# Scores as full 128-row products, a first stage with feature-major x and 768 columns, values' products spaced by eight steps

## The chip, the core and the metric

The kernel runs on one core of a Trainium2 chip. The metric is the device time of one execution in microseconds; a time is the median of several runs. Five engines work side by side, each in the order of its own stream: TensorE (PE in the profile; its weight loads are shown apart as PEld), VectorE (DVE), ScalarE (ACT), GpSimd (POOL) and SyncE (SP), which here issues every DMA.

## What is computed

Two layers of a hybrid block on 1,024 tokens of width 2,048, in float32. Cut to what matters here:

```python
mod = silu(c) @ w_mod + b_mod                    # 2048 -> 6144
shift, scale, gate = split(mod, 3)
h = rms_norm(x, g_pre) * (1 + scale) + shift
proj = h @ w_in                                  # 2048 -> 5648, split into ten parts
# a: 16 query heads on 4 key heads of 64, rotary on 16 of 64, window of 128, sinks
scores = einsum('bnqgrd,bnkgd->bngrqk', qb, kb) * 64 ** -0.5     # key blocks n-1 and n
m = maximum(max(where(valid, scores, -inf)), sink);  p = exp(scores - m)
y_a = einsum('bngrqk,bnkgd->bnqgrd', p / (sum(p) + exp(sink - m)), vb)
# b: chunked spatial gating;  c: gated linear attention in chunks, with a normed output
y = concat(y_a, y_b, y_c) * silu(z)
x = x + gate * rms_norm(y @ w_out, g_post)       # then the second layer
```

## The kernel before

The tokens are cut into two halves of 512, and a **phase** is one layer on one half: four phases, each with an input part (`in_phase`, ten groups of products with `w_in`) and an output part (`out_phase`). A product of two float32 matrices is made as three TensorE products in the fp32r format: both operands are split into a high and a low part (ACT casts, DVE subtracts; L368/L369 for weights, L278/L279 for activations), and high x high, high x low and low x high are added up in one PSUM bank. `mm_f` (L382 to L384) gives features on partitions, `mm_t` (L390 to L392) gives tokens on partitions. Weights pass in slices of two 128-row tiles through `wraw` (two raw buffers) and `whl` (three split ones). One **step** is one call of `mm_f` or `mm_t`, three products; after each, `tick()` lets the side work go on.

**The side work** is written as generators that are stepped between products. Each `yield n` says after how many steps it goes on. The lane "att" holds the attention, "gla" the gated linear attention, "sg" the spatial gating, "mod" the later modulation, which DVE does. `drain` runs a lane to a given point at once. Within this, a scheduler may move an instruction ahead of others that aren't ready, and `urgent()` raises priorities; an engine then keeps the resulting order. All side products share two PSUM buffers, `mx`; the ten groups have six, `pj`. Temporary tiles `t2` have four buffers.

**Attention** (L477 to L556): for each of the eight head pairs of a phase, `bp` runs over two pairs of token blocks. The queries of a head are held as 64 rows of high and 64 rows of low parts (`qs`), so one 128-row product with the high keys `kh` (L493) gives high x high and low x high, and a 64-row product with the low keys `kl` (L497) adds high x low. `kl[j]` holds the keys of two heads, one in each half of the partitions. After the evictions (L503/L505 on ACT, L506 on DVE) come the softmax (L511 to L525), 14 steps later the transposes of the probabilities (L538) and their products with the masks (L540, on DVE), and `LAG["t"]` steps after each of the two the next piece: three steps between the two heads, five before the products with the values (L551). The attention of the second set of heads starts when that of the first is drained, at the end of the group q1. In the step that follows, the gated part loads its norm weights (L823) and multiplies by them on DVE (L825, L827) before its own transposes on TensorE (L563).

**The first stage** (L1011 to L1129) makes the modulation of layer 0 and the first group of phase 0 together. Silu of c is held as 32 equal columns (`scb`); 64 modulation tiles of 512 KB (`wm0`, nine buffers) give 128 products of 32 columns (L1112), 16 in each of eight chunks, on the four column quarters of one PSUM bank. After a chunk, ACT copies the sums, TensorE transposes them (L197), DVE adds them up and makes the columns `acol` and `bcol` for two 128-row tiles of activations (L199 to L205). x comes with tokens on partitions (`xg`): ACT squares it for the norm (L1059), POOL multiplies it by 1/rms (L283), TensorE transposes it (L1089), DVE applies the columns (L1091), and `split` makes the two parts. Each of the 16 activation tiles is then multiplied by five 128-column weight tiles: the four of the group kcq and the first half of the key weights of part c. The other half follows as a group of its own (`proj_f(P, slots)`, L785). The rotary tables of the half (`rope_tables`, 18 DVE operations with two sines on ACT) are emitted before the first products.

Of the kernel before, what the change touches and what calls it, by code (L numbers as in the profile page):

```python
# [21 lines left out]
P = 128  # L22
# [3 lines left out]
NH = 2  # L26
# [6 lines left out]
LAG = {"s": (3, 4), "e": 14, "t": (3, 5)}  # L33
# [3 lines left out]
WM0 = 9  # L37
# [3 lines left out]
def hybrid_kernel(ctx: ExitStack, tc: tile.TileContext, a, y_out):  # L41
# [82 lines left out]
    def rsqrt(out, src, n):  # L124

        i = sm.tile([P, n], I32, tag="rq_i", name="rq_i")
# [3 lines left out]
        for it in range(3):  # L130
            w = sm.tile([P, n], F32, tag="rq_w", name="rq_w")
            V.tensor_tensor(w, yv, yv, ALU.mult)
            V.scalar_tensor_tensor(w, w, -0.5, src, ALU.mult, ALU.mult)
            dst = out if it == 2 else sm.tile([P, n], F32, tag="rq_y", name="rq_y")
            V.scalar_tensor_tensor(dst, w, 1.5, yv, ALU.add, ALU.mult)
            yv = dst
# [156 lines left out]
    def h_filler_x(h, slots):  # L293
# [3 lines left out]
        def fetch():  # L297
            if len(xs) < NK:
                xt = io_tile()
                load(xt, a["x_f"][len(xs)])  # L300
# [152 lines left out]
    def split_keys(j, kr, first):  # L453
# [23 lines left out]
    def attention(l, h, g0, qt, vt, cst):  # L477
# [5 lines left out]
        for m in range(4):  # L483
# [3 lines left out]
            for bp in range(2):  # L487
                sps = [mxt().rearrange("p (b k) -> p b k", b=2) for _ in range(2)]
                for b in range(2):
                    n = 2 * bp + b  # L490
                    k0 = P if h == 0 and n == 0 else 0
                    for p in range(2):
                        PE.matmul(sps[p][:, b, k0:], lhsT=qs[:, p, n * P:(n + 1) * P],  # L493
                                  rhs=kh[2 * j + p][:, n * P + k0:n * P + 256], start=True, stop=False)
                    for p in range(2):
                        rows = slice(64 * p, 64 * p + 64)
                        PE.matmul(sps[p][:, b, k0:], lhsT=qs[rows, p, n * P:(n + 1) * P],  # L497
                                  rhs=kl[j][rows, n * P + k0:n * P + 256], start=False, stop=True)
# [256 lines left out]
    def in_phase(l, h, slots, pre=None):  # L755
# [29 lines left out]
        ps = ps[4:] + proj_f(P, slots) if pre else proj_f(256, slots)  # L785
        ck = evac(2, hold, ps)
# [213 lines left out]
    for l, h in phases:  # L1000
        G_ = [(a["w_in"][l, k], 512) for k in range(len(GROUPS))]
        seq = [G_[0], (a["w_ck"][l], 256), (a["w_vcg"][l], 272)] + G_[1:]
        if (l, h) == (0, 0):
            seq = [(a["w_ck"][l, :, :, P:], P)] + seq[2:]
# [7 lines left out]
    with tc.tile_pool(name="start", bufs=1) as st:  # L1012
        scb = st.tile([P, NK, 32], F32, name="scb")
        V.tensor_copy(scb, sc.unsqueeze(2).broadcast_to([P, NK, 32]))
        xg = [st.tile([P, 4, NT, P], F32, name=f"x0_{g}") for g in range(4)]
        ss0 = sm.tile([P, NT, 4], F32, tag="xss4", name="xss4")
        load(mb[0], a["b_mod_col"][0])
        load(gpc[0], a["g_pre"][0])
# [255 lines left out]
```

## Time and profile before

| | |
|---|---|
| time, median of 3 runs | 3167.28 us (3166.84 to 3167.59) |
| the profiled execution | 3170.71 us, its span 3169.0 us |
| HBM traffic | 429.37 MB read, 36.70 MB written |
| DMA engines, mean share | 47.8% |
| granted TensorE clock, mean | 0.99 |

A row of a timeline gives start, duration, engine, line, operation, output and input by the program's names, and the count of merged instructions; in brackets, the idle time before it and what ended that. The program issues a float32 product as two instructions, so that a pair of modulation products shows as x4. TensorE's durations overlap: the step from one start to the next is what a product costs. Idle time of an engine that isn't the bound costs nothing.

The 40 slices of the page show where DVE and the DMAs are loaded, and the clock in the first one:

```profile
DVE  3268777665676877745355676644346475653425
PEclk8999999999999999999999999999999999999999
DMA  9754446566676335544346322334446322333535
```

### The profile page before, as it was taken

To read this page: it belongs to the slowest core of one execution; us is meant where nothing else is said; L and a number is where in the kernel's file an instruction comes from. 1 tells how busy PE (TensorE), PEld (TensorE's weight loads), DVE (VectorE), ACT (ScalarE), POOL (GpSimd) and SP (SyncE) were. 2 spreads that over 40 slices of the span, in tenths; PEclk is the share of its full clock that TensorE was granted. 3 is DMA by queue.
4 is the path that set the end of the run, shared out by engine and by line. 5 is a ranking of instruction groups with operands and counts; after the bars stand their busy time and mean duration, and the time that the engine had idled before them with its cause. 6 is when DMAs were issued, how large, how long until landed. Compare 5 with 4: busy or idle time off the path is not lost.

```text
span 3169.0 us, 44364 instructions
## 1 busy us (share of the span) xinstructions
PE 3095.0 (98%) x17346; PEld 2459.1 (78%) x17346; DVE 1838.1 (58%) x2953; ACT 1207.0 (38%) x2399; POOL 41.3 (1%) x80
## 2 busy tenths in 40 slices
PE   6999999999999999999999999999999999999998
PEld 2477777888878777888888877788888877788886
DVE  3268777665676877745355676644346475653425
ACT  3144437332344444323234454432223544432323
POOL 2000000000000000000000000000000000000000
PEclk8999999999999999999999999999999999999999
DMA  9754446566676335544346322334446322333535
GB/s 330 231 162 135 134 129 194 184 194 205 199 232 193 118 115 164 181 142 149 120 120 188 94 75 89 111 112 135 121 125 203 97 83 84 103 120 111 165 103 167
DMA packets 224195, 468.99 MB, mean 148 GB/s; under 512 B 21584, under 2 KB 77296, under 8 KB 223984
## 3 DMA queue, kind: packets, MB, share of 16 engines
q1 hardware_dynamic: 223984, 466.15, 47.8%
q8 instruction: 136, 2.23, 0.3%
q14 instruction: 75, 0.61, 0.1%
HBM read 429.37 MB, written 36.70 MB: 147 GB/s over the span
## 4 chain that ended last, share of the span: by engine, by line
PE 82%; DVE 7%; DMA 7%; ACT 2%; issue 2%; SPq 0%; DVEq 0%; ACTq 0%
PE pj L382 13%; PE pj L383 12%; PE pj L384 12%; PE pj L390 12%; PE pj L392 11%; PE pj L391 11%; DMA wm<-in_w_mod_dram 4%; PE mx L551 2%; PE mx L497 2%; PE mx L493 1%; PE pj L1112 1%; DVE ma L225 1%; DVE whl L369 1%; DMA t<-in_gla_norm_g_dram 1%; PE mx L538 1%
## 5 line engine op out<-in xcount | busy, mean ns | idle before, releaser
L369 DVE TENSOR_TENSOR whl<-wraw,whl 128x1024 fp32r<-128x1024 f32 (+3 forms) x512 | 590.9, 1154 | 740.7 <-ACT whl L368 739.0
L368 ACT CAST whl<-wraw 128x1024 fp32r<-128x1024 f32 (+3 forms) x512 | 509.0, 994 | 1108.3 <-PE pj L392 508.5
L390 PE MATMUL pj<-whl,act 128*128 128x512 f32 (+1 forms) x2048 | 792.2, 387 | 1.4 <-ACT whl L368 1.0
L392 PE MATMUL pj<-whl,act 128*128 128x512 f32 (+1 forms) x2048 | 779.7, 381 | 0.0
L391 PE MATMUL pj<-whl,act 128*128 128x512 f32 (+1 forms) x2048 | 777.5, 380 | 1.1 <-DVE whl L369 1.1
L382 PE MATMUL pj<-act,whl 128*128 128x512 f32 x1904 | 753.8, 398 | 3.6 <-ACT whl L368 1.9
L384 PE MATMUL pj<-act,whl 128*128 128x512 f32 x1904 | 745.6, 392 | 1.3 <-DVE whl L369 1.2
L383 PE MATMUL pj<-act,whl 128*128 128x512 f32 x1904 | 744.8, 391 | 0.3 <-DVE act L279 0.3
L390 PEld LDWEIGHTS pj<-whl,act 128*128 128x128 f32 x2048 | 386.1, 189 | 79.6 <-issue 6.0
L392 PEld LDWEIGHTS pj<-whl,act 128*128 128x128 f32 x2048 | 386.1, 189 | 73.9 <-issue 0.7
L391 PEld LDWEIGHTS pj<-whl,act 128*128 128x128 f32 x2048 | 386.6, 189 | 69.7 <-DVE whl L369 1.7
L382 PEld LDWEIGHTS pj<-act,whl 128*128 128x128 f32 x1904 | 357.5, 188 | 103.9 <-issue 20.4
L384 PEld LDWEIGHTS pj<-act,whl 128*128 128x128 f32 x1904 | 358.0, 188 | 85.5 <-issue 7.3
L383 PEld LDWEIGHTS pj<-act,whl 128*128 128x128 f32 x1904 | 358.4, 188 | 77.4 <-issue 5.9
L225 DVE SCALAR_TENSOR_TENSOR ma<-wm,sc,ma 128x512 f32<-128x512 f32 x240 | 179.8, 749 | 107.6 <-DMA wm<-in_w_mod_dram 105.2
L522 ACT ACTIVATE M<-M,at_nm 128x128 f32<-128x128 f32 x256 | 99.4, 390 | 47.6 <-DVE at_nm L514 45.1
L506 DVE COPY_PREDICATED M<-pmask,mx 128x256 f32<-128x256 uint8 x128 | 51.6, 443 | 91.4 <-ACT M L505 79.0
L540 DVE TENSOR_TENSOR PT<-mx,amask 128x1024 f32<-128x1024 f32 x64 | 78.0, 1220 | 24.3 <-PE mx L538 24.2
L1112 PE MATMUL pj<-wm,scb 128*32 128x512 f32 x256 | 66.8, 666 | 24.5 <-DMA wm<-in_w_mod_dram 24.5
L505 ACT COPY M<-mx 128x256 f32<-128x256 f32 x96 | 32.0, 375 | 133.0 <-PE mx L497 132.9
L551 PE MATMUL mx<-PT,v 128*64 128x128 f32 x960 | 67.9, 287 | 12.1 <-DVE PT L540 12.1
L551 PEld LDWEIGHTS mx<-PT,v 128*64 128x64 f32 x960 | 57.2, 143 | 26.7 <-DVE PT L540 14.8
(229 smaller groups left out, 2391.4 us busy)
## 6 DMA issues: line engine op xcount, KB each, us to landing
wraw<-in_w_in_dram SPq DMA_DIRECT2D x312, 512.0 KB, 3.6
wraw<-in_w_out_dram SPq DMA_DIRECT2D x136, 512.0 KB, 3.6
wm<-in_w_mod_dram SPq DMA_DIRECT2D x256, 256.0 KB, 3.3
wm<-in_w_mod_dram SPq DMA_DIRECT2D x64, 512.0 KB, 6.2
y<-at SPq DMA_DIRECT2D x64, 256.0 KB, 2.6
q<-y SPq DMA_DIRECT2D x64, 256.0 KB, 3.3
q<-x SPq DMA_DIRECT2D x36, 256.0 KB, 2.8
wraw<-in_w_vcg_dram SPq DMA_DIRECT2D x32, 272.0 KB, 2.8
```

Source lines behind the costliest of these rows:

```text
L225: V.scalar_tensor_tensor(acc, ws[k], sc[:, k:k + 1], acc, ALU.mult, ALU.add)
L368: S.copy(hl[:, 0], raw)
L369: V.tensor_tensor(hl[:, 1], raw, hl[:, 0].bitcast(F32), ALU.subtract)
L382: PE.matmul(ps, lhsT=whi, rhs=slot[:, 0], start=(k == 0), stop=False)
L383: PE.matmul(ps, lhsT=whi, rhs=slot[:, 1], start=False, stop=False)
L384: PE.matmul(ps, lhsT=wlo, rhs=slot[:, 0], start=False, stop=(k == NK - 1))
L390: PE.matmul(ps, lhsT=slot[:, 0, c], rhs=whi, start=(k == 0), stop=False)
L391: PE.matmul(ps, lhsT=slot[:, 0, c], rhs=wlo, start=False, stop=False)
L392: PE.matmul(ps, lhsT=slot[:, 1, c], rhs=whi, start=False, stop=(k == NK - 1))
L522: S.activation(Mf[:, k], Mf[:, k], AF.Exp, bias=nm[:, k:k + 1], scale=0.125, accum_out=den[:, k:k + 1])
L551: PE.matmul(yp[64 * p:64 * p + 64, n * P:(n + 1) * P], lhsT=vv[:, g * 64:g * 64 + 64], rhs=pts[p][:, w, n], start=(w == 0), stop=(w == 1 o ...
L1112: PE.matmul(mps[r:r + 32, :], lhsT=scb[:, k], rhs=w[:, kk], start=(k < 4), stop=(k >= 12))
```

## The change

Three edits, which the diff shows with their core.

1. **Scores.** The low keys get a tile for each head, `kl[g]`, whose other 64 partitions are set to zero once. The product with the low keys is then 128 rows high as well, with the same `qs` as the one with the high keys, and stands right behind it.
2. **First stage.** x comes with features on partitions (`x_f`, now for both halves of the tokens), two tiles in one load, ahead of the modulation. The squares are added up by TensorE products with ones (L1057), and 1/rms is made on DVE for 512 columns at once. Scaling, columns and split are three operations per tile (`fill`). The modulation tiles have twelve buffers; a chunk's products are emitted in two blocks of eight with projection steps between them. Each activation tile meets six weight tiles (768 columns), so the group of its own for the c-keys' second half goes. The rotary tables are emitted after chunk 1.
3. **Spacing.** `LAG["t"]` goes from (3, 5) to (3, 8).

```diff
-LAG = {"s": (3, 4), "e": 14, "t": (3, 5)}
+LAG = {"s": (3, 4), "e": 14, "t": (3, 8)}
-WM0 = 9
+WM0 = 12
...
-        if not first:
-            V.tensor_copy(kl[j][:, 0:P], kl[j][:, H:H + P].bitcast(F32))
-        for p in range(2):
-            r = slice(64 * p, 64 * p + 64)
-            V.tensor_tensor(kl[j][r, P:], kr[r], kh[2 * j + p][r, P:].bitcast(F32), ALU.subtract)
+            if not first:
+                V.tensor_copy(kl[g][r, 0:P], kl[g][r, H:H + P].bitcast(F32))
+            V.tensor_tensor(kl[g][r, P:], kr[r], kh[g][r, P:].bitcast(F32), ALU.subtract)
...
                     for p in range(2):
-                        PE.matmul(sps[p][:, b, k0:], lhsT=qs[:, p, n * P:(n + 1) * P],
-                                  rhs=kh[2 * j + p][:, n * P + k0:n * P + 256], start=True, stop=False)
-                    for p in range(2):
-                        rows = slice(64 * p, 64 * p + 64)
-                        PE.matmul(sps[p][:, b, k0:], lhsT=qs[rows, p, n * P:(n + 1) * P],
-                                  rhs=kl[j][rows, n * P + k0:n * P + 256], start=False, stop=True)
+                        for part, keys in enumerate((kh, kl)):
+                            PE.matmul(sps[p][:, b, k0:], lhsT=qs[:, p, n * P:(n + 1) * P],
+                                      rhs=keys[2 * j + p][:, n * P + k0:n * P + 256], start=(part == 0), stop=(part == 1))
...
-        ps = ps[4:] + proj_f(P, slots) if pre else proj_f(256, slots)
-        ck = evac(2, hold, ps)
+        ck = evac(2, hold, ps[4:] if pre else proj_f(256, slots))
...
+        xq = [act_p.tile([P, 2, H], F32, tag="act", name="xq") for _ in range(8)]
+        for c in range(8):
+            load(xq[c], a["x_f"][0, 2 * c:2 * c + 2].rearrange("j p t -> p j t"))
...
+        def mod_load(c, qs=range(8)):
+            if c < 8:
+                for q in qs:
+                    w = st.tile([P, 2, 512], F32, name="wm0", bufs=WM0)
+                    load(w, a["w_mod"][0, c, :, 2 * q:2 * q + 2])
+                    ws.append(w)
+        mod_load(0)
         first_load(0)
-        for g in range(4):
-            for t in range(NT):
-                S.activation(junk_tile().rearrange("p (j c) -> p j c", j=4), xg[g][:, :, t], AF.Square,
-                             accum_out=ss0[:, t, g:g + 1])
-        finish_stats(0, 0, ss0)
-        psk = [pjt() for _ in range(5)]
-        mps = pjt()
+        mod_load(1, range(4))
+
+
+        sums = mxt()
+        for c in range(8):
+            sq = st.tile([P, 2, H], F32, name="sq", bufs=2)
+            S.activation(sq, xq[c], AF.Square)
+            s2 = st.tile([P, H], F32, name="s2", bufs=2)
+            V.tensor_tensor(s2, sq[:, 0], sq[:, 1], ALU.add)
+            PE.matmul(sums, lhsT=ones, rhs=s2, start=(c == 0), stop=(c == 7))
+        r0 = st.tile([P, H], F32, name="r0")
+        V.tensor_scalar(r0, sums, 1.0 / D, EPS, ALU.mult, ALU.add)
+        rsqrt(r0, r0, H, st)
+        psk = [pjt() for _ in range(6)]
...
-                    for m in range(5):
+                    for m in range(6):
                         mm_f(psk[m], hls[m // 4], k2, m % 4, slots[k], k)
...
-        def tail(c, acc):
-
-            mod_columns(0, c, acc, 4)
-            yield
-            for j in (2 * c, 2 * c + 1):
-                pt = mxt()
-                for t in range(NT):
-                    PE.transpose(pt[:, t * P:(t + 1) * P], xg[j // 4][:, j % 4, t], ident)
-                v = t2()
-                V.tensor_scalar(v, pt, acol[0][:, j:j + 1], bcol[0][:, j:j + 1], ALU.mult, ALU.add)
-                slots.append(split(v))
-                yield
...
+        def columns(c, mps):
             acc = st.tile([P, 512], F32, name="mod_acc", bufs=2)
+            S.copy(acc, mps)
+            mod_columns(0, c, acc, 4)
+
+        def fill(c):
+            for j in range(2):
+                k = 2 * c + j
+                xt, b = t2(), bcol[0][:, k:k + 1]
+                V.scalar_tensor_tensor(xt, xq[c][:, j], acol[0][:, k:k + 1], r0, ALU.mult, ALU.mult)
+                s = act_p.tile([P, 2, 512], F32R, tag="act", name="act")
+                S.activation(s[:, 0], xt, AF.Identity, bias=b)
+                V.scalar_tensor_tensor(s[:, 1], xt, b, s[:, 0].bitcast(F32), ALU.add, ALU.subtract)
+                slots.append(s)
...
+        for c in range(8):
+            mps = mxt()
+            mod_products(mps, 0)
+            if c:
+                go(5)
+            mod_load(c + 1, range(4, 8))
+            if c == 0:
+                first_load(1)
+            mod_products(mps, 1)
+            mod_load(c + 2, range(4))
             with urgent():
-                S.copy(acc, mps)
-            go(2)
-            rest = tail(c, acc)
-            if c in (0, 7):
-                for _ in rest:
+                columns(c, mps)
+                fill(c)
+            if c:
+                go(7)
+            if c == 1:
+                for _ in rope_tables(0):
                     pass
+        go(12)
         for _ in todo:
             pass
...
-    kl = [pools["kk"].tile([P, P + H], F32R, name=f"kl{j}") for j in range(2)]
+
+    kl = [pools["kk"].tile([P, P + H], F32R, name=f"kl{g}") for g in range(4)]
+    for g in range(4):
+        G.memset(kl[g][64 - 64 * (g % 2):P - 64 * (g % 2)].bitcast(F32), 0.0)
```

What this does to the order of the instructions is shown at three places. A row gives the line, the operation, output and input, the size of the operand that is streamed and, where a row stands for several alike, their number; the program issues each product of float32 as two instructions, which such a row counts once.

**Scores, on TensorE**, the end of the first head pair's scores in phase 0. `kh` and `kl` are the high and low keys, `pj` a projection's bank, `act` and `whl` split activations and weights; L390 to L392 are projection products. Before:

```order
L493 MATMUL mx<-kh_1195,qs 128x128
L493 MATMUL mx<-kh_1196,qs 128x128
L497 MATMUL mx<-kl_1199,qs 128x128 x2
L493 MATMUL mx<-kh_1195,qs 128x256
L493 MATMUL mx<-kh_1196,qs 128x256
L497 MATMUL mx<-kl_1199,qs 128x256 x2
L390 MATMUL pj<-whl,act 128x512
```

With the change, the second half of that pair:

```order
L492 MATMUL mx<-kh_1167,qs 128x256
L492 MATMUL mx<-kl_1171,qs 128x256
L492 MATMUL mx<-kh_1168,qs 128x256
L492 MATMUL mx<-kl_1172,qs 128x256
L492 MATMUL mx<-kh_1167,qs 128x256
L492 MATMUL mx<-kl_1171,qs 128x256
L390 MATMUL pj<-whl,act 128x512
```

Each head now has its own low keys, and products with high and low keys alternate; both are 128 rows high.

**First stage, on TensorE**, behind the modulation of chunk 2 (counted from 0). L197 transposes its sums, L1089 transposes tiles of x, L1112 and L1087 are modulation products, L382 to L384 the first group's projection products. Before:

```order
L197 MATMUL mx<-ident,mod_acc 128x128 x4
L382 MATMUL pj<-act,hl_b 128x512
L1112 MATMUL pj<-wm_444,scb 32x512 x2
L383 MATMUL pj<-act,hl_b 128x512
L384 MATMUL pj<-act,hl_b 128x512
L1089 MATMUL mx<-ident,x_1_170 128x128
L1112 MATMUL pj<-wm_448,scb 32x512 x2
L1089 MATMUL mx<-ident,x_1_170 128x128 x7
L1112 MATMUL pj<-wm_463,scb 32x512 x2
L382 MATMUL pj<-act,whl 128x512 x3
```

With the change:

```order
L197 MATMUL mx<-ident,mod_acc 128x128 x4
L1087 MATMUL mx<-wm_395,scb 32x512 x2
L1087 MATMUL mx<-wm_397,scb 32x512 x2
L1087 MATMUL mx<-wm_399,scb 32x512 x2
L1087 MATMUL mx<-wm_401,scb 32x512 x2
L1087 MATMUL mx<-wm_509,scb 32x512 x2
L1087 MATMUL mx<-wm_511,scb 32x512 x2
L1087 MATMUL mx<-wm_513,scb 32x512
L382 MATMUL pj<-act,whl 128x512 x4
```

Where the rest of the chunk before and eight transposes of x, with two modulation pairs among them, stood between the transposes of the sums and the chunk's first projection product, six and a half pairs of the next chunk's modulation now stand.

On DVE, L158 to L176 are the rotary tables and L205 makes `acol`, the last of a chunk's columns. Before, behind chunk 0's columns:

```order
L205 SCALAR_TENSOR_TENSOR acol_103<-mod_t,gpc_109 128x2
L158 CAST t_196<-t_196 128x512
L159 TENSOR_SCALAR t_196<-t_196,fcol 128x512
L163 TENSOR_SCALAR t_200<-t_196 128x512
L164 TENSOR_SCALAR t_200<-t_200 128x512
```

With the change, the end of the rows between chunk 2's columns and the scaling of its first tile (L1098), which its first projection product needs:

```order
L164 TENSOR_SCALAR t_463<-t_463 128x512
L170 SCALAR_TENSOR_TENSOR t_455<-t_451,t_455 128x512
L165 TENSOR_SCALAR t_463<-t_463 128x512
L173 TENSOR_SCALAR t_455<-t_455 128x512
L168 SCALAR_TENSOR_TENSOR t_467<-t_463,t_447 128x512
L174 TENSOR_SCALAR t_455<-t_455 128x512
L1098 SCALAR_TENSOR_TENSOR t_546<-xq,acol_103,r_256 128x512
```

The tables have moved from behind chunk 0's columns to behind chunk 2's: fourteen of their operations, eight of them ahead of these rows, stand between L205 and L1098.

**Second attention of phase 0.** On TensorE, `PT` are the masked transposed probabilities, `v` the values, and `ident,hold` marks the transposes of the gated part. Before, its values' products and those transposes:

```order
L551 MATMUL mx<-PT,v 64x128
L390 MATMUL pj<-whl,act 128x512
L391 MATMUL pj<-whl,act 128x512
L551 MATMUL mx<-PT,v 64x128 x13
L392 MATMUL pj<-whl,act 128x512
L563 MATMUL mx<-ident,hold 128x128
```

With the change:

```order
L558 MATMUL mx<-ident,hold 128x128 x2
L390 MATMUL pj<-whl,act 128x512
L391 MATMUL pj<-whl,act 128x512
L392 MATMUL pj<-whl,act 128x512
L546 MATMUL mx<-PT,v 64x128 x14
L558 MATMUL mx<-ident,hold 128x128 x4
```

On DVE, `t_3930` and `t_3801` are the loaded norm weights. Before, around the head pair's second mask product:

```order
L540 TENSOR_TENSOR PT<-mx,amask 128x1024
L825 SCALAR_TENSOR_TENSOR hold<-hold,t_3930 128x512
L540 TENSOR_TENSOR PT<-mx,amask 128x1024
L827 TENSOR_TENSOR hold<-hold 128x512
L825 SCALAR_TENSOR_TENSOR hold<-hold,t_3930 128x512
```

With the change:

```order
L535 TENSOR_TENSOR PT<-mx,amask 128x1024
L225 SCALAR_TENSOR_TENSOR ma<-wm,sc,ma 128x512
L819 SCALAR_TENSOR_TENSOR hold<-hold,t_3801 128x512 x2
L821 TENSOR_TENSOR hold<-hold 128x512
L369 TENSOR_TENSOR whl<-wraw,whl 128x1024
L821 TENSOR_TENSOR hold<-hold 128x512
L819 SCALAR_TENSOR_TENSOR hold<-hold,t_3801 128x512
L225 SCALAR_TENSOR_TENSOR ma<-wm,sc,ma 128x512
L821 TENSOR_TENSOR hold<-hold 128x512
L535 TENSOR_TENSOR PT<-mx,amask 128x1024
```

The values' products have moved behind eight of the transposes, the first of which stands 31 projection products behind the end of q1's group, and the second mask product behind three of the gated part's products with the weights. The first attention of the phase, for its part, is still drained at the end of q1: in phases 1 to 3 its last softmax is followed by that end after 40 projection products, where it was 54.

More of the change, by code (lines that the diff above doesn't have):

```diff
@@ L123, in hybrid_kernel, with rsqrt @@
     load(fcol, a["k_fcol"])
-    def rsqrt(out, src, n):
-        i = sm.tile([P, n], I32, tag="rq_i", name="rq_i")
+    def rsqrt(out, src, n, pool=sm):
+        i = pool.tile([P, n], I32, tag="rq_i", name="rq_i")
         V.tensor_scalar(i, src.bitcast(I32), 1, None, ALU.logical_shift_right)
@@ L130, in rsqrt @@
         for it in range(3):
-            w = sm.tile([P, n], F32, tag="rq_w", name="rq_w")
+            w = pool.tile([P, n], F32, tag="rq_w", name="rq_w")
             V.tensor_tensor(w, yv, yv, ALU.mult)
             V.scalar_tensor_tensor(w, w, -0.5, src, ALU.mult, ALU.mult)
-            dst = out if it == 2 else sm.tile([P, n], F32, tag="rq_y", name="rq_y")
+            dst = out if it == 2 else yv
             V.scalar_tensor_tensor(dst, w, 1.5, yv, ALU.add, ALU.mult)
@@ L299, in fetch @@
                 xt = io_tile()
-                load(xt, a["x_f"][len(xs)])
+                load(xt, a["x_f"][1, len(xs)])
                 xs.append(xt)
@@ L1012, in hybrid_kernel @@
     with tc.tile_pool(name="start", bufs=1) as st:
+        load(mb[0], a["b_mod_col"][0])
+        load(gpc[0], a["g_pre"][0])
+        xq = [act_p.tile([P, 2, H], F32, tag="act", name="xq") for _ in range(8)]
+        for c in range(8):
+            load(xq[c], a["x_f"][0, 2 * c:2 * c + 2].rearrange("j p t -> p j t"))
         scb = st.tile([P, NK, 32], F32, name="scb")
         V.tensor_copy(scb, sc.unsqueeze(2).broadcast_to([P, NK, 32]))
[L1015 to L1018, printed above, removed]
         ws = deque()
@@ L1024, in first_load @@
                 k = slice(c * KC, (c + 1) * KC)
-                pool, tag = (st, "raw_a") if c % 3 == 2 else (wraw_p, "wraw")
-                r = pool.tile([P, KC, 512], F32, tag=tag, name="raw_a")
+                r = wraw_p.tile([P, KC, 512], F32, tag="wraw", name="raw_a")
                 load(r, a["w_in"][0, 0, :, k])
                 raw_a.append(r)
-                r = st.tile([P, KC, P], F32, name="raw_b", bufs=3)
-                load(r, a["w_ck"][0, :, k, 0:P])
+                r = st.tile([P, KC, 256], F32, name="raw_b", bufs=2)
+                load(r, a["w_ck"][0, :, k])
                 raw_b.append(r)
@@ L1034, in first_split @@
             if c < 8:
-                for raw, hls, cols in ((raw_a, hl_a, 512), (raw_b, hl_b, P)):
+                for raw, hls, cols in ((raw_a, hl_a, 512), (raw_b, hl_b, 256)):
                     r = raw.popleft()
-                    if cols == P:
-                        hl = st.tile([P, 2, KC, P], F32R, name="hl_b", bufs=2)
+                    if cols == 256:
+                        hl = st.tile([P, 2, KC, cols], F32R, name="hl_b", bufs=2)
                     else:
-                        hl = whl_p.tile([P, 2, KC, 512], F32R, tag="whl", name="whl")
+                        hl = whl_p.tile([P, 2, KC, cols], F32R, tag="whl", name="whl")
                     S.copy(hl[:, 0], r)
```

45 lines of the change are left out of this document (11 added, 34 removed).

## The prediction

> **What bounds the kernel now.** I read the page first, then the list of TensorE's waits, then the timeline of TensorE at the three places that the change touches.
>
> ```profile
> span 3169.0 us, 44364 instructions
> PE 3095.0 (98%) x17346; PEld 2459.1 (78%) x17346; DVE 1838.1 (58%) x2953; ACT 1207.0 (38%) x2399; POOL 41.3 (1%) x80
> PE 82%; DVE 7%; DMA 7%; ACT 2%; issue 2%; SPq 0%; DVEq 0%; ACTq 0%
> ```
> ```profile
> PE pj L1112 <- DMA wm<-in_w_mod_dram: 24.5, 6, 12.1
> PE mx L551 <- DVE PT L540: 12.1, 5, 4.2
> ```
>
> TensorE (PE) is the bound almost everywhere: busy 98% of the span, 82% of the chain that ended last. It is not busy for 74 us in all (3169.0 - 3095.0), of which 24.5 are the wait for modulation weights in the first stage, the longest line of the list, and 12.1 the wait of the values' products (L551) for DVE's mask product. So a microsecond taken out of TensorE's own stream shortens the kernel by nearly one, as long as DVE, at 58%, keeps up. Each term below is therefore a change of TensorE's stream or of its waits.
>
> **The scores.** Each of 32 head pairs has 16 score products, 512 in all. The first group of rows is a run of eight, the second a run of four (one of the two heads), then the counts, then three products of 272 columns elsewhere.
>
> ```profile
> 1054.06 0.39 PE L392 MATMUL pj<-whl,act 128*128 128x512 f32 x1
> 1054.29 0.40 PE L493 MATMUL mx<-kh,qs 128*128 128x256 f32 x2
> 1054.62 0.39 PE L497 MATMUL mx<-kl,qs 64*128 64x256 f32 x2
> 1054.93 0.50 PE L493 MATMUL mx<-kh,qs 128*128 128x256 f32 x2
> 1055.37 0.39 PE L497 MATMUL mx<-kl,qs 64*128 64x256 f32 x2
> 1055.68 0.50 PE L390 MATMUL pj<-whl,act 128*128 128x512 f32 x1
> 1056.02 0.40 PE L391 MATMUL pj<-whl,act 128*128 128x512 f32 x1
> ```
> ```profile
> 1050.35 0.33 PE L493 MATMUL mx<-kh,qs 128*128 128x256 f32 x1
> ...
> 1051.55 0.50 PE L390 MATMUL pj<-whl,act 128*128 128x512 f32 x1
> ```
> ```profile
> L493 PEld LDWEIGHTS mx<-kh,qs x256: 186/188/334, 271.8 to 2784.7; 128*128 128x128 f32 x128
> L493 PE MATMUL mx<-kh,qs x256: 218/282/580, 271.8 to 2784.8; 128*128 128x256 f32 x105, 128*128 128x128 f32 x23
> L497 PE MATMUL mx<-kl,qs x256: 322/381/579, 272.1 to 2785.0; 64*128 64x256 f32 x106, 64*128 64x128 f32 x22
> ```
> ```profile
> 190.18 0.29 PE L391 MATMUL pj<-whl,act 128*128 128x272 f32 x1
> 190.30 0.29 PE L392 MATMUL pj<-whl,act 128*128 128x272 f32 x1
> 190.43 0.29 PE L390 MATMUL pj<-whl,act 128*128 128x272 f32 x1
> ```
>
> A product of 512 columns lets the next one start after 0.23 us (1054.06 to 1054.29), one of 272 columns after 0.125, each with a weight load of its own. Score products have 256 columns, yet every change between a 128-row and a 64-row product takes some 0.31 from start to start, and the first 512-column product after a run holds its successor back by 0.34 instead of 0.23. A run of eight costs 1.39 + 0.11 = 1.50, a run of four 1.20 + 0.11 = 1.31. Counted through the timeline (271.83 to 2785.3) there are 46 whole runs of eight, 29 of four, and 28 products in broken runs, at some 0.2 each: 69 + 38 + 6 = 113 us. The change makes all 512 products 128 rows high. Nearest row: 0.125 x 256/272 = 0.118, so 512 x 0.118 = 60 (products of 128 columns taken at the same price). **Minus 53.** Ends: 0.114 (half of 0.23), with the 64 short products at half, gives 55 and minus 58; a weight load of 0.188 that is not hidden gives 96 and minus 17. I take 0.118, since the 272-column rows hide their loads.
>
> Here a rule speaks against the change. The Trainium skill, TensorE: Matmul & The Clock Gate, Part 3, says that products of few rows in different row groups run at the same time; by that rule alone the 64-row pairs are half price and the change adds 128 x 0.118 = 15 us. The Trainium skill, TensorEngine Tiling (Array Packing), Key Properties, says that changing the tiling mode drains the engine; by that one they can cost more than they save. The rows above agree with the second and only partly with the first: two 64-row products do share 0.31, but two full-row ones without a switch would need 0.24.
>
> The other edits here are small: four more 64-partition copies in each phase after the first of a layer, and four fills on POOL, which is busy 1%. I cost them at nothing.
>
> **The first stage.** Rows in order of time: the landing of modulation tiles, the wait for x, the first projection product, a modulation pair among projections, two pairs together, the wait before the transposes, the end of the stage; then DVE and the groups that price the new chain.
>
> ```profile
> 14.23 1.05 PE L1112 MATMUL pj<-wm,scb 128*32 128x512 f32 x4 [0.24 <-DMA wm<-in_w_mod_dram]
> 15.51 1.05 PE L1112 MATMUL pj<-wm,scb 128*32 128x512 f32 x4 [0.23 <-DMA wm<-in_w_mod_dram]
> ...
> 30.03 4.48 PE L1112 MATMUL pj<-wm,scb 128*32 128x512 f32 x12 [12.06 <-DMA wm<-in_w_mod_dram]
> ...
> 46.01 1.20 PE L382 MATMUL pj<-act,whl 128*128 128x512 f32 x4
> ...
> 140.50 0.40 PE L382 MATMUL pj<-act,hl_b 128*128 128x512 f32 x1
> 140.82 1.05 PE L1112 MATMUL pj<-wm,scb 128*32 128x512 f32 x4
> 141.81 0.50 PE L383 MATMUL pj<-act,hl_b 128*128 128x512 f32 x1
> 142.14 0.40 PE L384 MATMUL pj<-act,hl_b 128*128 128x512 f32 x1
> 142.47 1.07 PE L1112 MATMUL pj<-wm,scb 128*32 128x512 f32 x8
> 144.32 0.66 PE L197 MATMUL mx<-ident,mod_acc 128*128 128x128 f32 x4 [0.79 <-ACT mod_acc L1122]
> ...
> 183.88 0.77 PE L390 MATMUL pj<-whl,act 128*128 128x272 f32 x4 [1.00 <-ACT whl L368]
> ```
> ```profile
> 18.01 0.17 DVE L199 TENSOR_REDUCE mod_m<-mx 128x4 f32<-128x16 f32 x1 [14.01 <-PE mx L197]
> ...
> 27.00 0.43 DVE L158 CAST t<-t 128x512 f32<-128x512 int32 x1 [8.36 <-DMA t<-in_positions_dram]
> ...
> 34.10 0.42 DVE L174 TENSOR_SCALAR t<-t 128x512 f32<-128x512 f32 x1
> ```
> ```profile
> L317 DVE SCALAR_TENSOR_TENSOR q<-q,acol,hold 128x512 f32<-128x512 f32 x16 | 11.8, 747 | 5.4 <-DMA q<-in_x_f_dram 5.4
> L320 ACT ACTIVATE act<-q,bcol 128x512 fp32r<-128x512 f32 x16 | 11.6, 722 | 9.8 <-PE pj L392 6.8 <-DVE q L317 3.0
> ```
>
> Start: tiles of 512 KB land 1.28 us apart, the eighth at 15.5. With x ahead, x is there at 15.5 and the first chunk's eighth tile at 15.5 + 8 x 1.28 = 25.8. Squares, sums and the 12 operations of 512 columns for rstd (at most 0.75 each, 9.0) end near 27.5; the columns are ready near 29 (pair 1.0, copy and transposes 1.5, DVE's four small ones 0.65), so they cover rstd; beyond 1.5 us it would show. Two more steps of 0.75 and 0.72 put the first projection product at 31, not 46.
>
> From there to the end: 288 products x 0.23 = 66. Of 56 modulation pairs, 30 stand alone in the new order (1.31 - 0.23 + 0.10 = 1.18 each: 35.4) and 26 adjoin another (two together 1.07 plus the switches, 1.2: 15.6). Seven transposes with their wait cost 1.2 each: 8. The 64 transposes of x, and POOL's 16 scalings of x before them, go. Sum 125, and the end at 156 without waits.
>
> New waits: in the old order transposes and pairs stand between a chunk's columns and its first projection; in the new one little or nothing does. The chain of reduce, two steps and activation is about 2.2 us: I read 2.3 for chunk 1, 1 each for chunks 5 and 6, 3.4 for chunk 7 (two weight splits come between). In chunk 2 the 14 rope operations now stand on DVE between the columns and the first scaling (34.52 - 27.00 = 7.5), and ACT's table load and sine stand before its activation: 7 after the 6.5 pairs that cover some. That is 15, and the end at 171.
>
> ```profile
> 20.00:40.00 20.00, 4.87 (x14) 0.74 (x16) 11.89 (x30) 14.86 (x35) 0.00 (x0) 0.62 0.89 329
> ```
>
> After its long idle stretch TensorE was granted 0.62 of its clock. Each new wait of over 2 us may cost 1 to 2 us of slow products; I add 3 in all. End near 174, against 182.9 (183.88 less its wait). The half of the c-keys that ran as a group of its own is within both ends, so nothing else is saved. **Minus 9.** Ends: minus 18 (chunk 2's wait hidden, no slow clock) and plus 4 (the two cosine and sine stores on SP's queue also hold back the modulation loads behind them until the sines are done, so that every later chunk starts late).
>
> **The spacing.** The largest waits of the values' products look removable, but see what ends them.
>
> ```profile
> 456.79 0.60 PE L538 MATMUL mx<-ident,M 128*128 128x128 f32 x4
> 468.53 3.11 PE L551 MATMUL mx<-PT,v 128*64 128x128 f32 x26 [4.16 <-DVE PT L540]
> ```
> ```profile
> 466.65 0.69 DVE L825 SCALAR_TENSOR_TENSOR hold<-hold,t 128x512 f32<-128x512 f32 x1 [5.42 <-DMA t<-in_gla_norm_g_dram]
> ```
>
> DVE itself is waiting for a load, of the gated part's norm weights, with the second mask product queued behind. The new order puts the values' products past that, but the transposes of L558, which need L821's product behind the same load, now come first, 31 products after the group's end at 456.79: there at about 464.6, while DVE has their input at 466.65 + 2.0 = 468.7. A wait of 4.1 takes the place of 4.2. Behind it on TensorE stand the projections of sv, and the evictions on ACT and DVE that wait for these. The three other phases have the same place: the other waits of the line come to 8 together (12.1 less 4.16), and now, 27 products after the group's end, I read about 3.5 each. **Plus 3**; ends minus 17 (all of the 12.1 and the slow clock behind it gone) and plus 6.
>
> Last, the first attention of a phase takes 12 steps more, and its end is forced at the end of q1's projection: its last softmax is followed after 40 products (9 us) rather than 54 in three phases. I add **4** for that and for a DVE that is pressed harder (0 to 15).
>
> Sum: -53 - 9 + 3 + 4 = -55. Against the profiled execution (3170.7, its span 3169.0) that is 3116; the median of the runs shown is 3.4 lower, 3167.3, so the forecast is **3112**.
>
> **Rivals.**
> - *Given back to DVE* (0.12): the attention becomes bound by DVE and ACT, and half of the 53 returns as waits for L501 and L533: 3139. For it: DVE is at 58% over the span and higher in these slices; against: the list of waits runs from the longest down, and 12.1 is already its longest line on DVE.
> - *The spacing works as meant* (0.08): DVE or the load is earlier than I think; minus 17 instead of plus 3: 3092.
> - *The first stage gives nothing* (0.1): plus 4 instead of minus 9: 3125.
> - *Slower* (0.04): 0.31 belongs not to the change of rows but to alternating key tiles in one accumulation. Then all 512 products keep 0.30 (1.20/4) and nothing runs side by side: 154 instead of 113, so plus 41 where I have minus 53: 3206. It decides from a mean spacing of 0.23, where 512 products cost what they cost now. Against it: after a run the delay also reaches L390 and L391, which touch no keys. It is also where the first of the two rules would lead.
> - *No effect of the scores' edit*: excluded by the order, in which eight products of 128 rows stand together.
>
> **How the numbers follow.** My own case has 0.66. The range 3084 to 3140 takes in the ends of the first stage and the spacing, and the first three rivals; outside stay the slower one and the ends of the scores. 0.2% (6 us) is about what a measurement of this kernel can tell from no change: faster 0.94, within 0.02, slower 0.04.
>
> **What would show it.** Scores: runs of eight in about 0.95 us, and no 0.34 behind them. First stage: first projection near 31, first 272-column product near 174, one wait of some 7 us near 75. Spacing: L546 without a wait, L558 with one of 3 to 4 in each phase. I am wrong if score products stand over 0.15 apart, if waits on L501 or L533 pass 20 us, or if the first stage ends after 185.

## The result, and the profile after

The changed kernel takes **3138.0 us** (3137.0 to 3140.2, four runs); the kernel before took 3167.4 in the same comparison. The ratio is 0.9892 (95% interval 0.9878 to 0.9906). The forecast was a gain of 55 us. Between the two medians lie 29; the ratio makes it 34 (30 to 39), and in the later comparisons, where the kernel before has medians of 3172.5, 3172.0 and 3171.2, 3138.0 is also 33 to 35 less. The single edits below are set against 34. The time of 3138 lies at the upper edge of the range. The page of the changed kernel, its span, engines and chain:

```profile
span 3135.9 us, 44198 instructions
PE 3044.2 (97%) x17298; PEld 2448.4 (78%) x17298; DVE 1845.5 (59%) x2956; ACT 1198.4 (38%) x2367; POOL 24.1 (1%) x68
PE 80%; DMA 8%; DVE 7%; ACT 3%; issue 2%; SPq 0%; DVEq 0%; ACTq 0%
```

TensorE's own work shrank by 51 us (3095.0 to 3044.2), and 18 of them came back as idle time (74.0 to 91.7). The list of TensorE's waits says where, with the sum, the number and the longest of each:

```profile
PE mx L558 <- DVE hold L821: 17.1, 4, 5.1
PE pj L382 <- ACT act L1100: 16.6, 6, 6.2
PE mx L1057 <- DVE s L1056: 8.2, 1, 8.2
PE mx L492 <- DVE hold L617: 7.2, 6, 4.3
PE mx L533 <- DVE M L520: 5.0, 4, 2.7
...
PE mx L546 <- DVE PT L535: 0.8, 1, 0.8
```

The 24.5 us of waits for modulation tiles are gone but for 0.9, the values' 12.1 but for 0.8. In their place stand the new first stage's own wait for activations (L1100), its start, and the gated part's transposes (L558).

**Scores.** A run of eight, from TensorE's timeline:

```profile
2755.24 0.39 PE L392 MATMUL pj<-whl,act 128*128 128x512 f32 x1
2755.47 0.28 PE L492 MATMUL mx<-kh,qs 128*128 128x256 f32 x1
2755.58 0.28 PE L492 MATMUL mx<-kl,qs 128*128 128x256 f32 x1
...
2756.30 0.28 PE L492 MATMUL mx<-kl,qs 128*128 128x256 f32 x1
2756.42 0.40 PE L390 MATMUL pj<-whl,act 128*128 128x512 f32 x1
2756.65 0.40 PE L391 MATMUL pj<-whl,act 128*128 128x512 f32 x1
```

Score products now start 0.12 us apart, a run of eight takes 0.95 (2755.47 to 2756.42), and L391 follows L390 after 0.23 instead of 0.34. Over the trace the score products, each counted to the start of the next product without waits, went from 106.1 to 66.3 us. More than 512 x 0.118 = 60 remains because single runs are longer: the one at 302.1 us takes 1.63 at a granted clock of 0.54, some others 1.15 to 1.24.

**First stage**, in order of time, then the granted clock (the number after POOL's) in its first three stretches:

```profile
30.77 0.79 PE L382 MATMUL pj<-act,whl 128*128 128x512 f32 x1 [2.27 <-ACT act L1100]
...
54.76 0.79 PE L382 MATMUL pj<-act,whl 128*128 128x512 f32 x1 [2.27 <-ACT act L1100]
...
85.50 2.08 PE L382 MATMUL pj<-act,whl 128*128 128x512 f32 x4 [6.24 <-ACT act L1100]
...
168.34 2.07 PE L382 MATMUL pj<-act,whl 128*128 128x512 f32 x4 [3.29 <-ACT act L1100]
...
179.27 0.29 PE L390 MATMUL pj<-whl,act 128*128 128x272 f32 x1
```
```profile
30.77:54.76 23.99, 21.71 (x73) 8.46 (x73) 5.04 (x11) 3.44 (x6) 0.00 (x0) 0.86 1.03 407
54.76:85.50 30.74, 23.77 (x99) 9.46 (x99) 13.91 (x28) 6.64 (x9) 0.00 (x0) 0.83 0.39 130
```

The waits are where they were read from the order, and of the size; the products between them are slower than forecast, at 0.86 and 0.83 of the clock.

**Spacing.** The place in phase 1, on TensorE, then the operation on DVE that holds its input back, and the load behind which DVE stands (number of loads, size, median us to landing), beside another load of that size:

```profile
1225.33 0.45 PE L558 MATMUL mx<-ident,hold 128*128 128x128 f32 x1 [5.10 <-DVE hold L821]
1225.43 0.77 PE L390 MATMUL pj<-whl,act 128*128 128x512 f32 x1
1226.01 0.63 PE L391 MATMUL pj<-whl,act 128*128 128x512 f32 x1
```
```profile
1223.29 1.29 DVE L819 SCALAR_TENSOR_TENSOR hold<-hold,t 128x512 f32<-128x512 f32 x2 [5.05 <-DMA t<-in_gla_norm_g_dram]
```
```profile
wm<-in_w_mod_dram SPq DMA_DIRECT2D x256, 256.0 KB, 3.4
t<-in_gla_norm_g_dram SPq DMA_DIRECT2D x4, 256.0 KB, 8.8
```

The wait has moved from L551 to L558, as forecast, and behind it, for about 3 us, products stand some 0.42 apart (1226.01 to 1226.43) instead of 0.23.

How the difference to before builds up is read from one landmark in each phase, the start of its first 272-column product (before: 183.88, 957.86, 1728.84 and 2477.43; after: 179.27, 942.79, 1711.62 and 2452.72) and the two spans. Each column is the change of one stretch in one profiled execution, in us. Such a value has a spread of its own: five kernels with the same first stage end it between 174.96 and 179.29.

| kernel | first stage | phase 0 | phase 1 | phase 2 | phase 3 |
|---|---|---|---|---|---|
| changed kernel | -4.6 | -10.5 | -2.2 | -7.5 | -8.4 |
| before, scores only | 0.0 | -9.5 | -12.1 | -10.2 | -10.7 |
| before, spacing only | -0.2 | -5.5 | +7.3 | +4.2 | +3.7 |
| before, first stage only | -6.9 | -10.6 | +13.0 | -0.3 | -0.1 |
| changed, spacing of five | -4.6 | -13.8 | +0.1 | -10.3 | -10.5 |

### The profile page after: what moved, and what is told of

The parts are those of the page before. It is cut to its first block, busy times and chain, and to the rows that moved or that the text cites. A ratio compares the mean times of both kernels' runs of the same rounds, so it can differ in the third digit from the quotient of the medians.

```text
span 3135.9 us, 44198 instructions
## 1 busy us (share of the span) xinstructions
PE 3044.2 (97%) x17298; PEld 2448.4 (78%) x17298; DVE 1845.5 (59%) x2956; ACT 1198.4 (38%) x2367; POOL 24.1 (1%) x68
## 4 chain that ended last, share of the span: by engine, by line
PE 80%; DMA 8%; DVE 7%; ACT 3%; issue 2%; SPq 0%; DVEq 0%; ACTq 0%
PE pj L382 13%; PE pj L384 12%; PE pj L383 12%; PE pj L390 11%; PE pj L391 11%; PE pj L392 11%; DMA wm<-in_w_mod_dram 3%; PE mx L492 2%; DVE whl L369 1%; PE mx L1087 1%; PE mx L546 1%; DMA t<-in_gla_norm_g_dram 1%; DMA wm<-in_x_dram 1%; DVE ma L225 1%; ACT whl L368 1%
## 5 line engine op out<-in xcount | busy, mean ns | idle before, releaser
L369 DVE TENSOR_TENSOR whl<-wraw,whl 128x1024 fp32r<-128x1024 f32 (+2 forms) x504 | 587.1, 1165 | 709.7 <-ACT whl L368 707.0
L368 ACT CAST whl<-wraw 128x1024 fp32r<-128x1024 f32 (+2 forms) x504 | 505.7, 1004 | 1158.6 <-PE pj L392 616.0
L390 PE MATMUL pj<-whl,act 128*128 128x512 f32 (+1 forms) x2048 | 785.9, 384 | 0.2 <-ACT q L763 0.2
L391 PE MATMUL pj<-whl,act 128*128 128x512 f32 (+1 forms) x2048 | 780.2, 381 | 0.2 <-DVE whl L369 0.2
L392 PE MATMUL pj<-whl,act 128*128 128x512 f32 (+1 forms) x2048 | 778.8, 380 | 0.0
L382 PE MATMUL pj<-act,whl 128*128 128x512 f32 x1888 | 751.2, 399 | 23.6 <-ACT act L1100 16.6
L384 PE MATMUL pj<-act,whl 128*128 128x512 f32 x1888 | 739.4, 392 | 2.0 <-DVE whl L369 1.7
L382 PEld LDWEIGHTS pj<-act,whl 128*128 128x128 f32 x1888 | 356.2, 189 | 121.5 <-issue 21.0
L392 PEld LDWEIGHTS pj<-whl,act 128*128 128x128 f32 x2048 | 386.8, 189 | 72.2 <-issue 1.1
L390 PEld LDWEIGHTS pj<-whl,act 128*128 128x128 f32 x2048 | 387.1, 189 | 70.7 <-issue 2.3
L391 PEld LDWEIGHTS pj<-whl,act 128*128 128x128 f32 x2048 | 387.4, 189 | 68.0 <-issue 1.6
L384 PEld LDWEIGHTS pj<-act,whl 128*128 128x128 f32 x1888 | 355.9, 188 | 87.8 <-issue 9.4
L225 DVE SCALAR_TENSOR_TENSOR ma<-wm,sc,ma 128x512 f32<-128x512 f32 x240 | 179.7, 749 | 112.1 <-DMA wm<-in_w_mod_dram 109.7
L501 DVE COPY_PREDICATED M<-pmask,mx 128x256 f32<-128x256 uint8 x128 | 51.6, 442 | 68.6 <-ACT M L500 52.7
L535 DVE TENSOR_TENSOR PT<-mx,amask 128x1024 f32<-128x1024 f32 x64 | 77.4, 1217 | 10.9 <-PE mx L533 10.5
L492 PE MATMUL mx<-kh,qs 128*128 128x256 f32 (+1 forms) x256 | 68.5, 298 | 8.7 <-DVE hold L617 7.2
L492 PE MATMUL mx<-kl,qs 128*128 128x256 f32 (+1 forms) x256 | 66.6, 285 | 0.0
L492 PEld LDWEIGHTS mx<-kh,qs 128*128 128x128 f32 x256 | 49.4, 194 | 21.3 <-issue 9.9
```

The costliest lines, as they stand in the source:

```text
L225: V.scalar_tensor_tensor(acc, ws[k], sc[:, k:k + 1], acc, ALU.mult, ALU.add)
L368: S.copy(hl[:, 0], raw)
L369: V.tensor_tensor(hl[:, 1], raw, hl[:, 0].bitcast(F32), ALU.subtract)
L382: PE.matmul(ps, lhsT=whi, rhs=slot[:, 0], start=(k == 0), stop=False)
L384: PE.matmul(ps, lhsT=wlo, rhs=slot[:, 0], start=False, stop=(k == NK - 1))
L390: PE.matmul(ps, lhsT=slot[:, 0, c], rhs=whi, start=(k == 0), stop=False)
```

## The edits one by one

Four kernels take the change apart; each follows from the diff above (the fourth sets `LAG["t"]` back to (3, 5) in the changed kernel).

> The kernel before with only the scores' edit (low keys per head, 128-row products). Theory: the score products themselves fall from 106 to 66 us as in the changed kernel's trace, and the projection products behind them lose 8 us more; with the spacing and the first stage of before nothing takes that back, so 3167 - 46 = 3121. Rival (given back to DVE): half returns as waits for the evictions and mask products, 3143. The waits of L551's successor line for the mask product stay near 12 under the theory and pass 20 under the rival.

Measured: ratio 0.9857 (0.9844 to 0.9871), 3126.9 us against 3172.5 in that comparison: **minus 46**. The scores' edit alone is faster than the whole change. In its waits L546 for the mask product has 13.5 us, against 12.1 before. Yet something was given back: TensorE's own time fell by 51.0 us (3095.0 to 3044.0), and its idle time rose by 8.4 (74.0 to 82.4), spread over several lines of waits for DVE.

> The kernel before with only the spacing of eight steps. Theory: the 12 us of waits of the values' products go, some 6 us of their slow products too, and waits of the gated part's transposes of 3 to 5 us in each phase take their place: within 4 us of before, 3167. Rival 1 (works as meant): 3150. Rival 2 (the longer attention of each half costs): 3175.

Measured: ratio 1.0035 (1.0023 to 1.0047): **plus 11**, outside the theory's 4 us and nearest to the second rival. Its list of waits shows the exchange:

```profile
PE mx L563 <- DVE hold L827: 11.3, 3, 4.1
...
PE mx L563 <- DVE PT L540: 4.0, 1, 4.0
```

These are 15.3 us of waits for L563 where L551 had 12.1, and L538 waits 3.5 for DVE where it had 0.4. In all, TensorE's idle time rose by 6.8 us and its own time by 2.6. Slower products are a part of it in phase 2, where waits rose by 1.9 (2.2 to 4.1 within the attention's stretch) and the `mm_t` products of that stretch took 2.5 more; in phase 1, where most was lost, waits rose by 4.0 (4.1 to 8.1) and these products took no more than before.

> The changed kernel with scores and spacing as before, so that the new first stage stands alone. Theory: its trace shows the first 272-column product at 179.3 instead of 183.9, so minus 4.6: 3163. Rival: minus 9 as predicted and the rest lost to the other edits, 3158.

Measured: ratio 0.9974 (0.9965 to 0.9983): **minus 8**, with the end of the stage at 176.99. That fits the rival's number, but not its reason: phase 0 gained another 10.6 and phase 1 lost 13.0.

> The changed kernel with the spacing back at five steps. Theory: the trade of one wait for another is nearly even, 3138 give or take 4, with the waits back at the values' products and gone from the gated part's transposes. Rival: the spacing is what ate the missing 20 us, 3120 to 3126. Second rival (it helps once the scores are short): 3148.

Measured: ratio 0.9865 (0.9852 to 0.9879): some 8 us below the changed kernel, between theory and rival. The spacing costs about as much beside the other edits as alone. The two lines of waits are even: 17.9 us for the values' products with five steps, 17.1 for the gated part's transposes with eight. TensorE's idle time is 6.9 us longer with eight (91.7 against 84.8) because of other waits, the largest of them L382's for ACT's L436 with 4.3, which the five steps don't have. But 0.9865 is not below the 0.9857 of the scores alone: beside the scores, no gain of the new first stage can be told. In the table, the last row against that of the scores is 8.9 us ahead at the end of phase 0 and loses 12.2 in phase 1.

## What made the 64-row products slow

The kernel before, with the second block's products mirrored; the low keys keep their 64 rows:

```diff
-                    for p in range(2):
-                        PE.matmul(..., rhs=kh[2 * j + p][...], start=True, stop=False)
-                    for p in range(2):
-                        PE.matmul(..., rhs=kl[j][rows, ...], start=False, stop=True)
+                    for part in ((0, 1) if b == 0 else (1, 0)):
+                        for p in range(2):
+                            rows = slice(64 * p, 64 * p + 64) if part else slice(0, P)
+                            keys = kl[j] if part else kh[2 * j + p]
+                            PE.matmul(..., rhs=keys[rows, ...], start=(part == b), stop=(part != b))
```

> The kernel before with its 64-row products kept, but the second block's products mirrored (low keys first), so that a run of eight has two changes of row count instead of four; the sums are the same. Theory (the change of row count costs some 0.2 us each): a run of eight falls from 1.44 to about 1.05 us and a run of four from 1.17 to 0.8, 25 to 30 us less than before, ratio 0.991. Rival (a 64-row product is slow by itself, 0.26 each): no change, 1.000. Second rival (the alternation of key tiles costs): a third of the gain, 0.997.

Measured: ratio 0.9904 (0.9889 to 0.9919), **minus 30**, as the theory has it. A run of eight:

```profile
2695.94 0.40 PE L496 MATMUL mx<-kh,qs 128*128 128x256 f32 x2
2696.27 0.50 PE L496 MATMUL mx<-kl,qs 64*128 64x256 f32 x4
2696.70 0.50 PE L496 MATMUL mx<-kh,qs 128*128 128x256 f32 x2
2697.04 0.39 PE L390 MATMUL pj<-whl,act 128*128 128x512 f32 x1
2697.27 0.40 PE L391 MATMUL pj<-whl,act 128*128 128x512 f32 x1
```

It takes 1.10 us, and the product behind it has its 0.23 back: with two changes of row count fewer, 1.39 + 0.11 became 1.10, so a change costs 0.2. The Trainium skill, TensorEngine Tiling (Array Packing), Key Properties, says that a change of tiling mode drains the engine; these rows agree.

Four 64-row products together take 0.43 (2696.27 to 2696.70), but not one after another. A window that ends at 2696.269 holds one of them, and one that ends at 2696.272 holds two:

```profile
2696.27 0.39 PE L496 MATMUL mx<-kl,qs 64*128 64x256 f32 x2
```

The two products of a pair, one in each half of the rows, start at most 0.004 us apart (2696.267 and 2696.270, then 2696.490 and 2696.494), so they run side by side; in the kernel before as well (1054.616 and 1054.620). What TensorE: Matmul & The Clock Gate, Part 3, of the Trainium skill says of products in different row groups running together agrees with these starts. Three kernels then fit one sum, with 0.118 for a full-row product or a pair and 0.2 for a change. Eight products without a change make 0.94 (0.95 measured in the changed kernel), four full-row products, two pairs and two changes 1.11 (1.10 here), and the same with four changes 1.51 (1.50 before). So full height gives up the pairing, 0.24 us in a run of eight, and saves 0.8 of changes.

## The load behind the gated part

The norm weights go to tiles of their own, loaded ahead of the phases, in the changed kernel and in the one before:

```diff
-            gn = t2()
-            load(gn.rearrange("p (h d) -> p h d", h=4), a["gla_norm_g"][l:l + 1]...)
+            gn = gnorm[l]
```

> The changed kernel with the gated part's norm weights loaded once per layer ahead of the phases, into tiles of their own. In the changed kernel's trace the load of these weights takes 9.4 us to land and DVE stands 4.3 to 5.1 us behind it. Theory: this load alone causes the waits of the gated part's transposes (17.1 us) and the slow products behind them (about 1.5 us in each of four phases), so 20 to 24 us less than the changed kernel: ratio to before 0.982, 3115. Rival: the transposes wait for DVE's queue, not for the load; then other work of DVE takes its place and the time stays within 5 us of 3138.

Measured: ratio 0.9813 (0.9799 to 0.9828), against 0.9892 for the changed kernel: **25 us**. Of L558's waits those for DVE are gone from the list (1.7 us for ACT's L560 are left). TensorE's idle time fell by 14.4 us and its own time by 11.3, with the same 17298 products; the mean granted clock rose from 0.989 to 0.992.

> The kernel before with only the norm weights loaded ahead. Theory: the waits of the values' products for the mask product that stand behind that load (4.2, 2.9, 2.2 and 2.0 us, 11.3 in all) go, with some slow products behind them: 3153, ratio 0.9955. Rival: the mask product is late for other work of DVE, and the time stays within 4 us of before.

Measured: ratio 0.9945 (0.9933 to 0.9958), **minus 17**; the waits of L551 for the mask product are gone from its list. So the same load was what the kernel before waited for, and the spacing had moved its victim, not the cause.

## The first stage and the later modulation

> The changed kernel with the rotary tables emitted ahead of the sums of squares, as the kernel before has them. Theory: chunk 2's wait of 6.2 us and the slow clock behind it go, the first 272-column product comes near 172 instead of 179: 3130. Rival: the tables' DVE work delays 1/rms and with it the first projection product (30.8) by up to 7 us, and nothing is won: 3138.

The edit moves `rope_tables(0)` from behind chunk 1 to ahead of the sums of squares. Measured: ratio 0.9879 (0.9863 to 0.9894), not told apart from the changed kernel's 0.9892. Within the stage both sides were half right: the first projection product came 12 us later, at 42.9, and yet the first 272-column product stood at 169.7 instead of 179.3, since chunk 2 waits no more and the clock stays full. Of these 9.5 us, 4.8 were lost again in phase 1 (plus 2.6, against minus 2.2).

In phases 0 and 1 DVE also makes the later modulation (L225), whose tiles had two buffers; the next kernel gives them four (`("wm", 2)` to `("wm", 4)`).

> The changed kernel with four buffers instead of two for the later modulation's tiles. Theory: the 10 us that the changed kernel loses in phases 0 and 1 beyond the three edits taken alone come from DVE standing for a modulation tile at an unlucky place (at 1022 us it waits 2.1 us for one, and the gated part's scores' masks behind it make TensorE wait 4.3): with the tiles there in time 6 to 12 us less than the changed kernel, ratio 0.986. Rival: the tiles are late because of the DMA queue itself, not for lack of buffers, or because DVE has too much to do: within 3 us of 3138.

Measured: ratio 0.9833 (0.9819 to 0.9848), **some 18 us** below the changed kernel. Phase 0 went from minus 10.5 to minus 20.7 and phase 1 from minus 2.2 to minus 6.0; phases 2 and 3 stay within 0.6. The first stage ends 2.5 earlier, which these buffers can't have done, since L225 first runs behind it (at 188.17 in the changed kernel). The group of L225, of the changed kernel and then of this one, with its busy time, mean duration and idle time ahead of it:

```profile
L225 DVE SCALAR_TENSOR_TENSOR ma<-wm,sc,ma 128x512 f32<-128x512 f32 x240 | 179.7, 749 | 112.1 <-DMA wm<-in_w_mod_dram 109.7 <-DVE ma L225 0.3
```
```profile
L225 DVE SCALAR_TENSOR_TENSOR ma<-wm,sc,ma 128x512 f32<-128x512 f32 x240 | 179.9, 750 | 35.5 <-DMA wm<-in_w_mod_dram 31.7 <-DVE ma L225 0.4
```

DVE stood 110 us behind these loads, and 32 with four buffers; so the tiles were late mostly for lack of buffers. The place that the expectation named was the wrong one, though: the wait of 4.3 us of the scores behind L617 is still there (at 1024.48). The gain is spread over phases 0 and 1.

## All of it together

> The changed kernel with three corrections together: norm weights loaded at the start of each layer, four buffers for the later modulation's tiles, rotary tables emitted first. Theory (three separate waits, each with its own cause): the single gains against the changed kernel add up, 25 + 18 + 4 = 47 us: ratio to before 0.975, 3091. Rival (they share waits): the largest two thirds, ratio 0.979, 3105.

Measured: ratio 0.9751 (0.9738 to 0.9765), 3091.4 us. The three gains add up within their intervals (47 us expected, 45 measured by the ratios), so the large ones, 25 and 18, don't share their waits. The 4 of the tables, not told apart from nothing alone, stay unproven here.

> The same with the spacing back at five steps. Theory: the spacing cost 8.5 us in the changed kernel only because the transposes then met the load; with the load gone it costs nothing or helps, so this one is 0 to 8 us above the one with eight steps. Rival: the longer attention itself costs (its forced end at q1), and five steps are again some 8 us faster.

Measured: ratio 0.9733 (0.9720 to 0.9747), **3086.8 us**, the fastest of all, 84 below the kernel before in that comparison. The theory had it 0 to 8 us above the one with eight steps; the median is 4.6 below. The two intervals overlap, but no run with eight steps (3089.4 to 3097.9) was as short as the longest with five (3087.5): the spacing does not help even when the load is gone. What is left of TensorE's waits:

```profile
PE mx L1064 <- DVE s L1063: 8.4, 2, 8.3
PE pj L382 <- ACT act L1107: 8.4, 5, 3.3
PE mx L492 <- DVE hold L617: 6.7, 5, 4.2
...
PE mx L546 <- DVE PT L535: 1.4, 1, 1.4
```

> Spacing five, norm weights loaded at the start of each layer, four modulation buffers, scores of the change, and the first stage of before. Theory: the new first stage is worth what its own end shows (14 us with the tables first, 4.6 as in the changed kernel) once the later modulation no longer makes DVE stand at unlucky places, so this one is 10 to 15 us above the last. Rival: whatever the first stage gains is given back later, and the two are within 4 us.

Measured: ratio 0.9792 (0.9778 to 0.9805), 3105.7 us: with the norm weights loaded ahead and four buffers in both kernels, the new first stage, tables first, is worth 19 us, 15.8 of them at its own end (169.05 against 184.85), a little more than expected. Which of the two corrections lets the gain stay is not separated. A hint is in the ratios: this kernel is 21 us below the scores alone, and the norm weights brought 17 in the kernel before. If they bring as much here, the buffers are worth some 4 us beside the old first stage (an estimate; each of the three ratios has an interval of about 4 us to either side), against 18 beside the new one. No run has the four buffers alone beside the old stage.

## Why the forecast was 26 us too low

The pages of the profiled executions split each difference to the kernel before into TensorE's own time and its idle time, in us:

| kernel | own time | idle time |
|---|---|---|
| before, scores only | -51.0 | +8.4 |
| before, spacing only | +2.6 | +6.8 |
| before, first stage only | -3.0 | -1.9 |
| the three added up | -51.4 | +13.3 |
| changed kernel | -50.8 | +17.7 |
| changed, norm weights ahead | -62.1 | +3.3 |
| changed, four buffers | -57.6 | +7.8 |

- **Scores, minus 53.** Mechanism and size of the step hold: 0.95 for a run of eight, 0.34 back to 0.23, and 51.0 us less of TensorE's own time, of which the score products alone bring 41.5 (106.1 to 64.6). The edit alone is worth 46 (interval 41 to 50), because 8.4 came back as idle time; that belongs to the last term.
- **First stage, minus 9.** Its waits were forecast as 2.3, 7, 1, 1 and 3.4, and are 2.27, 6.24, 1.27, 1.27 and 3.29; the first projection product was forecast at 31 and came at 30.77. The end at 179.3 instead of 174 goes with the slow clock, for which 3 us were allowed. The kernel with norm weights loaded ahead runs this stage in the same order with the same waits of 2.27 and 6.25, was granted 0.92 and 0.97 there, and ends it at 174.96. Alone the stage is worth 8 (interval 5 to 11). That this is the number forecast is in part luck, for it is the sum of minus 17.5 up to the end of phase 0 and plus 13.0 in phase 1, which the forecast doesn't have.
- **Spacing, plus 3.** The step was right and its size was not: alone plus 11, in the changed kernel some 8. The waits of L558 came to 17.1 for 14.6 forecast, close enough; what was left out are waits of other lines (L538 alone, L382 for ACT's L436 in the changed kernel). The idle time is some 7 us longer both times, alone and in the changed kernel.
- **Give-back, plus 4.** This term was too small, and its mechanism was another. It looked for the loss in the attention's evictions, but in the changed kernel waits for L501 are 0.2 us and L533's come to 5.0. Idle time rose by 17.7 us in all, 8.4 of it with the scores alone. What DVE itself stood behind were loads: with the norm weights ahead 14.4 of the idle time go, with four buffers 9.9. The forecast read DVE's share of busy time and not that DVE stood 105 us behind the modulation's tiles already before:

```profile
L225 DVE SCALAR_TENSOR_TENSOR ma<-wm,sc,ma 128x512 f32<-128x512 f32 x240 | 179.8, 749 | 107.6 <-DMA wm<-in_w_mod_dram 105.2
```

- **Rivals.** The first one, given back to DVE, had 3139, and 3138 was measured; its number was met by luck, since the waits that it names, L501's and L533's, come to 5.2 us and not to half of 53. That the spacing works as meant is refuted, and that alternating key tiles cost as well: they stand 0.12 apart.

By the ratios the single edits are worth minus 46, minus 8 and plus 11, together minus 43, and the change minus 34. Open is what the 9 us between them are, and why phase 1 loses 13 us when the first stage alone is exchanged, that is, which of DVE's operations meet which tile. With norm weights ahead and four buffers the gain of the stage stays, but the places were not traced one by one.

## What to carry over

When TensorE waits for a DVE operation, look at what that operation's engine itself stood behind: here a load, and the longer distance between producer and consumer that was tried only moved the wait to the next one in line. Keep products that run in turn at one row count, or at least group them by it: two half-height products do run side by side, but a change of height cost more than that saves. And an edit whose gain shows at the end of its own stage isn't safe until the engine that works beside the next stages has its operands ahead of time.

## What was not expected of the hardware

The load of the norm weights, 128 values repeated four times in each of 128 partitions, took 8.8 us for 256 KB, while a load of 256 KB of modulation weights took 3.4 (median). A 512 KB load of projection weights that was issued 2.3 us behind it (442.49 against 440.16) landed after 8.4, where the median of these loads is 3.6. Two 64-row products start within 0.004 us of each other, and still a change between 64 and 128 rows costs 0.2. And one order of instructions is granted different clocks: 0.86 and 0.83 in one execution, 0.92 and 0.97 in another, for the same stretches of the first stage with the same waits, which moved its end by 4.3 us.
